# The scan's second round moved into the first group's end, and split products issued pass by pass

## The chip, the cores and the metric

The kernel runs on one core of a Trainium2 chip. The metric is device time in microseconds (us) of one execution. Before the change the median of 3 runs is 2160.34 us (2158.78 to 2164.11).

## The reference

One decoder layer runs over 2064 prompt positions (16 meta tokens and 2048 prompt tokens) and 8 short sequences of 8 tokens, model width 1024. All is float32. Cut to what matters:

```python
xn = rmsnorm(h, norm_gain);  proj = xn @ w_in          # u_s, z_s, u_p, z_p and two gates
dt = exp(log_dt);  abar = exp(dt * a)                   # 64 groups of 16 channels, 64 complex states each
s[t] = abar * s[t-1] + bbar @ u_s[t]                    # the linear scan over time (S5)
y_s = gelu(real(c @ s) + d * u_s);  y_s = y_s * sigmoid(y_s @ w_glu + b_glu)
y_p = ((window means of u_p) - u_p) @ pool_mix * pool_scale
merged = g_s * ((y_s * silu(z_s)) @ w_branch_ssm) + g_p * ((y_p * silu(z_p)) @ w_branch_pool)
out = rmsnorm(h + merged @ w_out)                       # and the final states of the scan
```

## The kernel before, in words

**Tiling.** Features lie on the 128 partitions, tokens along the free axis. The 2128 tokens are cut into four token groups g0 to g3 (`GROUPS`) of 544, 536, 536 and 512 columns; g0 drops its 16 meta tokens after the pooling inputs, so most of its products have 528 columns. In g0, g1 and g2 a product is too wide for one PSUM bank, so it has two token halves (`nh` = 2, 272, 268 or 264 columns); g3 has one of 512.

**Split products.** Each operand is kept as a high part and a low part in fp32r (`wh`, `wl` for weights, `ah`, `al` for activations). A product is three passes, high by high (L126), high weights by low activations (L127), low weights by high activations (L128), all added in the same PSUM tile `acc` (3 buffers). `mm3` issues the three for one half. `proj` goes over 8 blocks of 128 input features and calls `mm3` for each half: 48 matmuls for a group with two halves.

**Units.** The work is a written list of 339 units, most of them one `proj` with one block of 128x1024 weights. Around each unit the main loop converts the weights two units ahead (POOL writes `wh` at L103, DVE writes `wl` at L202), loads three units further, and issues the unit's *post* (the evacuation of `acc`) one unit later. Each engine runs its instructions in the order in which the loop issues them.

**Stages of a token group.** Pooling inputs and their gates (`up`, `zp`, `mix`), the pooling branch with its gate (`brp`, `gate`), the gate of the scan's branch (`zs`), `glu`, the scan's branch (`gate`, `brs`), and `out`. The scan's inputs (`us`) of all groups come early: g1 and g0 at the start, g2 and g3 in the middle of g0's work.

**The scan.** 64 channel groups are handled as 32 pairs, in two rounds: round 0 has the columns of g0 and g1 (135 steps of 8 tokens), round 1 those of g2 and g3 (123 steps and 8 sample sequences). A round is 37 *ticks*; in one tick six consecutive pairs are each moved on by one step. EARLY of a tick sits a quarter of its share into the unit, LATE at its end. Of the pair's steps, PE has L508 (into PSUM tile `sx`) and L573, L574 (into `sy`), float32 matmuls; ACT L499 to L501, L515, L516, L518, L542, L543 and L578 (`sy` to `sY`, one buffer, from which a DMA writes `ys`); DVE L495, L524, L533, L536 (twice), L553, L554; POOL L486, L489, L528, L563 to L566. `sx` and `sy` exist once each, so the next pair's matmul waits until the last one is evacuated.

**Where ticks go.** `spread` shares a round's 37 ticks out over a range of units, with weight `low` for units in the set `busy` and 1 elsewhere. Round 0 has one or two ticks in most units from g0's `brp` on (34 units). Round 1 starts in the first `gate` behind g0's `zs` and ends in g2's `brp`; the pooling units of g1 and g2 have weight `BB` = 0, and of the 12 + 20 + 5 ticks in g0, g1 and g2 a unit has at most one.

**Memory.** `to_ssm` opens the SBUF pool `sw` and the PSUM pool `ps` for the scan and keeps them to the end. `final_states` writes the final states out.

Of the kernel before, what the change touches and what calls it, by code (L numbers as in the profile page):

```python
# [15 lines left out]
PSUM = bass.MemoryType.PSUM  # L16
# [4 lines left out]
P = 128  # L21
# [36 lines left out]
XN = 5.5, 0.25  # L58
NPART = 2
LAST = 14  # L60
BA, BB = 0.25, 0.0
RAW = 3

BESIDE = [0] * 3 + [2] * 2 + [0] * 4 + [3] * 3 + [2] * 27
# [24 lines left out]
def hybrid_step(ctx, tc, a):  # L89
# [30 lines left out]
        flush()  # L120
        lows.append((l, x, h))

    def mm3(out, w, x, first, last):

        (wh, wl), (xh, xl) = w, x
        PE.matmul(out, wh, xh, start=first, stop=False)  # L126
        PE.matmul(out, wh, xl, start=False, stop=False)  # L127
        PE.matmul(out, wl, xh, start=False, stop=last)  # L128

    def rsqrt_mean(out, ss, r, q):  # L130

# [323 lines left out]
    sw = {}  # L455
# [148 lines left out]
    def between(part):  # L604

        while mid and mid[0][0] <= part:
            _, f, args = mid.pop(0)
            f(*args)


    class Group:
# [42 lines left out]
        def proj(self, w, xh, xl, halves=None, meta=False):  # L654


            ps = self.acc()
            n, km = (self.N, 0) if meta else (self.ND, self.km)
            if halves:
                n = self.HD  # L660
            strided = km and xh[0].shape[1] == self.C
            tn = T // self.nh
            nk = len(xh)
            for k in range(nk):
                between(k / nk)
                for h in halves or range(self.nh):
                    out = ps[:, h, :n]
                    if strided:
                        out = out.rearrange("p (t k) -> p t k", t=tn)
                        x = [v[k].rearrange("p (t k) -> p t k", t=T)[:, h * tn:(h + 1) * tn, km:]  # L670
                             for v in (xh, xl)]
                    else:
                        x = [v[k][:, h * n:(h + 1) * n] for v in (xh, xl)]
                    mm3(out, [x[:, k * P:(k + 1) * P] for x in w], x, k == 0, k == nk - 1)
            return ps

        def slot(self, pool, k, x, eng):
# [180 lines left out]
        def mix(self, wi, w):  # L858
            f0 = 2 * wi
            xh, xl = zip(self.pl.pop(f0), self.pl.pop(f0 + 1))  # L860
            pss = []
            for j in range(2):
                wj = []
                for x in w:
                    wj.append([x[:, k * 256 + j * P:k * 256 + (j + 1) * P] for k in range(2)])
                ps = self.acc()
                for k in range(2):
                    for h in range(self.nh):
                        c = slice(h * self.ND, (h + 1) * self.ND)
                        mm3(ps[:, h, :self.ND], (wj[0][k], wj[1][k]), (xh[k][:, c], xl[k][:, c]),  # L870
                            k == 0, k == 1)
                pss.append(ps)

            def post():
                for j in range(2):
                    fb = f0 + j
                    s = self.sz[fb]
                    V.scalar_tensor_tensor(self.v3(s), self.pv(pss[j]), psc16[:, fb:fb + 1], self.v3(s),  # L878
                                           ALU.mult, ALU.mult)
                for fb in (f0, f0 + 1):  # L880
                    self.yh[fb], self.yl[fb] = self.slot(self.sb, fb, self.sz.pop(fb), "a")
            return post
# [160 lines left out]
    def at(i, f, *args):  # L1043
        events.setdefault(max(i, 0), []).append((f, args))
# [29 lines left out]
    def u_pgate(g):  # L1074
        for f in range(NB):
            i = add("w", W_BRP + f, g.brp, f)
            if f + 3 < NB:
                add("w", W_GP + f + 3, g.gate, f + 3, 1)
        return i
# [72 lines left out]
    def spread(r, lo, hi, busy, low):  # L1152

        share = [low if i in busy else 1.0 for i in range(lo, hi)]
        total, done, n = sum(share), 0.0, 0
        for i, w in zip(range(lo, hi), share):
            done += w
            while n < NTICK and (n + 0.5) * total < done * NTICK:
                ticks.setdefault(i, []).append((r, n))
                n += 1  # L1160
# [22 lines left out]
    def to_ssm():  # L1183
        while beside():
            pass
        sw["g"] = ctx.enter_context(tc.tile_pool(name="gp", bufs=1))
        sw["p"] = ctx.enter_context(tc.tile_pool(name="sw", bufs=1))
        ps = ctx.enter_context(tc.tile_pool(name="ps", bufs=1, space=PSUM))
        for n in ("sx", "sy"):
            sw[n] = ps.tile([P, 2, 160], F32, name=n)  # L1190
        sw["xs"] = sw["p"].tile([P, GRP, NS], F32, name="xs")

    g0, g1, g2, g3 = grp
    for f in range(NB):
# [20 lines left out]
    i = len(units)  # L1215
# [5 lines left out]
    i = len(units)  # L1221
# [11 lines left out]
    for f in range(NB):  # L1233
# [7 lines left out]
        at(j, g0.y_split, f)  # L1241
        at(j + (f > 4), g0.y_gate, f)
    u_rest(g0, g1, 2)
    for g, nxt in ((g1, g2), (g2, g3), (g3, None)):
        n = len(units)
        u_pool(g)
        busy |= set(range(n, len(units)))
        hi = u_pgate(g)
        if g is g2:
            spread(rounds[1], i + 2, hi, busy, BB)  # L1250
        u_zs(g, range(NB), True)
        u_rest(g, nxt, 0)
    at(hi, final_states)


    V.memset(onesm, 1.0)
# [151 lines left out]
```

## Time and profile before

| | |
|---|---|
| median of 3 runs | 2160.34 us |
| the profiled execution | 2158.2 us, of which 2156.4 us is the span of its instructions |
| mean granted TensorE clock | 0.990 |
| HBM read, written | 242.32 MB, 40.62 MB |

The span is the time from the first to the last instruction of the profiled execution; busy time of an engine is counted within it. PE is TensorE's matmuls, PEld its weight loads, which overlap with matmuls, DVE VectorE, ACT ScalarE, POOL GpSimd, SP the queue that issues DMAs. A stretch is named by its start and end in us from the span's start. The units can be found in the trace by counting matmuls; they give these stretches:

| stretch, us | units | ticks |
|---|---|---|
| 290 to 577.5 | 34: g0's `brp` and `gate`, `zs` 0 to 4, `us` of g2 and g3 | 37 of round 0 |
| 577.5 to 805 | 35: the rest of g0 | 12 of round 1 |
| 805 to 930 | 23: g1's pooling inputs | none |
| 930 to 1286.5 | 53: the rest of g1 | 20 of round 1 |
| 1412.7 to 1482 | 11: g2's `brp` and `gate` | 5 of round 1 |
| 1482 to the end | 122: the rest of g2, and g3 | none |

### The profile page before, as it was taken

The page shows a single profiled execution, that of the slowest core. Times are in us where ns is not written, and L with a number is a line of the kernel's source. Part 1 is how long each engine was busy: PE and PEld are TensorE (multiplying, and loading weights), DVE is VectorE, ACT ScalarE, POOL GpSimd, SP SyncE. Part 2 cuts the span into 40 slices and gives each one's busy share as a digit, 9 for nine tenths or more (in the row PEclk, how much of TensorE's full clock was granted, in tenths as well). Part 3 has the DMA queues.
Part 4 walks back from the last instruction along what each step waited for, and adds up shares of the span by engine and source line. Part 5 has one row for each costly group of instructions (what it writes and reads, how often), then busy time and mean ns, then how long its engine had stood idle before and what let it go on. Part 6 is the DMA issues. An engine that isn't in the chain of part 4 may idle for free.

```text
span 2156.4 us, 37693 instructions
## 1 busy us (share of the span) xinstructions
PE 2084.8 (97%) x14968; PEld 1970.0 (91%) x14968; DVE 1395.2 (65%) x1916; ACT 686.5 (32%) x1243; POOL 931.2 (43%) x1054
## 2 busy tenths in 40 slices
PE   7999999889899999999999999999999999999998
PEld 7988899888799999999899999999999987888887
DVE  7889968978656686644856676634643767456444
ACT  3213357645444332144544332121210221112101
POOL 3387747655444452234644452233421333144222
PEclk9999999999999999999999999999999999999999
DMA  6646557586933543245444543234333433343233
GB/s 200 145 116 165 164 170 206 143 198 156 186 122 124 159 137 127 81 121 142 124 124 138 162 134 125 89 119 115 100 103 108 141 128 119 101 133 117 91 98 105
DMA packets 261279, 287.77 MB, mean 133 GB/s; under 512 B 106096, under 2 KB 203760, under 8 KB 261104
## 3 DMA queue, kind: packets, MB, share of 16 engines
q1 hardware_dynamic: 261104, 285.37, 45.8%
q8 instruction: 118, 1.93, 0.4%
q14 instruction: 57, 0.47, 0.1%
HBM read 242.32 MB, written 40.62 MB: 131 GB/s over the span
## 4 chain that ended last, share of the span: by engine, by line
PE 69%; DVE 7%; DMA 5%; ACT 3%; issue 2%; POOL 1%; SPq 0%; DVEq 0%; ACTq 0%; POOLq 0%
PE acc L126 22%; PE acc L128 22%; PE acc L127 22%; DMA ys<-sY 3%; DVE wl L202 1%; DVE sX L533 1%; DVE sph L554 1%; DVE sX L536 1%; PE sy L574 1%; PE sx L508 1%; DVE al L114 1%; PE sy L573 1%; DMA mat_d<-mp 1%; DVE sph L495 0%; ACT sXw L543 0%
## 5 line engine op out<-in xcount | busy, mean ns | idle before, releaser
L126 PE MATMUL acc<-ah,wh 128*128 128x268 f32 (+4 forms) x4504 | 1370.9, 304 | 8.9 <-ACT ah L698 6.6
L128 PE MATMUL acc<-ah,wl 128*128 128x268 f32 (+4 forms) x4504 | 1360.5, 302 | 4.8 <-DVE wl L202 4.8
L127 PE MATMUL acc<-al,wh 128*128 128x268 f32 (+4 forms) x4504 | 1359.0, 302 | 0.0
L126 PEld LDWEIGHTS acc<-ah,wh 128*128 128x128 f32 x4504 | 853.2, 189 | 43.2 <-issue 7.7
L128 PEld LDWEIGHTS acc<-ah,wl 128*128 128x128 f32 x4504 | 850.5, 189 | 33.1 <-DVE wl L202 5.9
L127 PEld LDWEIGHTS acc<-al,wh 128*128 128x128 f32 x4504 | 852.4, 189 | 27.5 <-issue 0.2
L103 POOL TENSOR_SCALAR wh<-raw 128x1024 fp32r<-128x1024 f32 (+1 forms) x336 | 395.9, 1178 | 964.2 <-PE acc L127 834.7
L202 DVE TENSOR_TENSOR wl<-raw,wh 128x1024 fp32r<-128x1024 f32 (+1 forms) x336 | 427.2, 1272 | 147.2 <-POOL wh L103 146.7
L890 ACT ACTIVATE sg<-acc,hb 128x536 f32<-128x536 f32 (+2 forms) x64 | 44.9, 702 | 404.0 <-PE acc L128 403.9
L524 DVE TENSOR_TENSOR sX<-sx,scc 128x270 f32<-128x270 f32 (+1 forms) x64 | 27.2, 424 | 106.5 <-ACT xs L518 66.3
L114 DVE TENSOR_TENSOR al<-H,ah 128x536 fp32r<-128x536 f32 (+3 forms) x96 | 88.4, 954 | 7.6 <-POOL ah L103 5.2
L946 DVE SCALAR_TENSOR_TENSOR H<-po,H 128x536 f32<-128x536 f32 (+2 forms) x32 | 25.4, 795 | 101.9 <-ACT po L944 101.9
L846 ACT ACTIVATE H<-acc 128x536 f32<-128x536 f32 (+2 forms) x64 | 39.0, 610 | 139.5 <-PE acc L128 139.1
L105 ACT ACTIVATE ah<-H 128x536 fp32r<-128x536 f32 (+3 forms) x80 | 50.7, 646 | 96.1 <-DVE H L878 77.4
L847 DVE SCALAR_TENSOR_TENSOR H<-H,acc 128x536 f32<-128x536 f32 (+2 forms) x64 | 44.8, 700 | 47.0 <-ACT H L846 46.5
L813 DVE TENSOR_TENSOR w<-E 128x483 f32<-128x483 f32 (+2 forms) x32 | 22.0, 687 | 74.2 <-POOL E L800 65.1
L573 PE MATMUL sy<-su,smc 128*128 128x135 f32 (+1 forms) x256 | 52.4, 286 | 18.1 <-ACT sY L578 15.1
L957 DVE SCALAR_TENSOR_TENSOR sg<-sg,acc 128x536 f32<-128x536 f32 (+2 forms) x32 | 22.4, 702 | 69.4 <-PE acc L128 69.4
L536 DVE TENSOR_TENSOR_SCAN sX<-r,state,sX 128x135 f32<-128x135 f32 (+1 forms) x128 | 65.6, 554 | 2.3
L944 ACT ACTIVATE po<-acc,hb 128x536 f32<-128x536 f32 (+2 forms) x32 | 22.5, 704 | 134.5 <-PE acc L128 134.5
L899 DVE SCALAR_TENSOR_TENSOR G<-sg,acc 128x536 f32<-128x536 f32 (+2 forms) x32 | 22.4, 700 | 64.2 <-PE acc L128 64.2
L574 PE MATMUL sy<-sS,smc 128*128 128x135 f32 (+1 forms) x256 | 53.4, 291 | 10.8 <-POOL sS L565 10.8
(232 smaller groups left out, 2271.0 us busy)
## 6 DMA issues: line engine op xcount, KB each, us to landing
raw<-in_wb SPq DMA_DIRECT2D x318, 512.0 KB, 3.8
smc<-mat_d SPq DMA_DIRECT2D x64, 256.0 KB, 4.1
smb<-mat_d SPq DMA_DIRECT2D x64, 128.0 KB, 3.2
xr<-in_xb SPq DMA_DIRECT2D x21, 268.0 KB, 4.3
H<-in_xb SPq DMA_DIRECT2D x19, 268.0 KB, 4.4
su<-us SPq DMA_DIRECT2D x32, 135.0 KB, 4.2
ys<-sY SPq DMA_DIRECT2D x32, 135.0 KB, 4.6
us<-po SPq DMA_DIRECT2D x16, 268.0 KB, 6.7
```

The costliest lines, as they stand in the source:

```text
L103: G.tensor_scalar(out, in_, 1.0, 0.0, ALU.mult, ALU.add)
L105: A.activation(out, in_, AF.Copy)
L114: V.tensor_tensor(l, x, h.bitcast(F32), ALU.subtract)
L126: PE.matmul(out, wh, xh, start=first, stop=False)
L127: PE.matmul(out, wh, xl, start=False, stop=False)
L128: PE.matmul(out, wl, xh, start=False, stop=last)
L202: V.tensor_tensor(l[:, c], r[:, c], h[:, c].bitcast(F32), ALU.subtract)
L536: V.tensor_tensor_scan(x[:, j], r8[:, i].to_broadcast([P, g.kp]), x[:, j], state[:, i], ALU.mult, ALU.add)
L573: PE.matmul(d["py"][:, j], d["m"][:, j, :P], d["u"][:, j], start=True, stop=False)
L574: PE.matmul(d["py"][:, j], d["m"][:, j, P:], d["S"][:, j], start=False, stop=True)
L847: V.scalar_tensor_tensor(self.v3(out), self.v3(out), 1.0, self.pv(ps), ALU.add, ALU.mult)
L890: A.activation(self.v3(s), self.pv(ps), AF.Tanh, scale=0.5, bias=hb[:, b, fb:fb + 1])
```

## The change

There are two edits. First, `mm3` takes all halves of a product at once: the first pass runs over both halves, then the second over both, then the third. For g3, and for the last units of g3's `out`, which have one half each, the order stays.

Second, round 1's 37 ticks are spread over the units from g0's `zs` 7 to `out` 6, the first 8 of the range with weight `BB` = 0.5. The ticks in g1 and g2 are gone. `final_states` comes at g1's first unit instead of g3's last `brp`, and one unit later `end_ssm` closes the scan's PSUM and SBUF pools. No later code takes memory from what they held.

```diff
--- before.py
+++ after.py
@@ -58,7 +58,7 @@
 XN = 5.5, 0.25
 NPART = 2
 LAST = 14
-BA, BB = 0.25, 0.0
+BA, BB = 0.25, 0.5
 RAW = 3
 
 BESIDE = [0] * 3 + [2] * 2 + [0] * 4 + [3] * 3 + [2] * 27
@@ -120,12 +120,16 @@
         flush()
         lows.append((l, x, h))
 
-    def mm3(out, w, x, first, last):
-
-        (wh, wl), (xh, xl) = w, x
-        PE.matmul(out, wh, xh, start=first, stop=False)
-        PE.matmul(out, wh, xl, start=False, stop=False)
-        PE.matmul(out, wl, xh, start=False, stop=last)
+    def mm3(outs, w, xs, first, last):
+
+
+        wh, wl = w
+        for out, (xh, _) in zip(outs, xs):
+            PE.matmul(out, wh, xh, start=first, stop=False)
+        for out, (_, xl) in zip(outs, xs):
+            PE.matmul(out, wh, xl, start=False, stop=False)
+        for out, (xh, _) in zip(outs, xs):
+            PE.matmul(out, wl, xh, start=False, stop=last)
 
     def rsqrt_mean(out, ss, r, q):
 
@@ -663,6 +667,7 @@
             nk = len(xh)
             for k in range(nk):
                 between(k / nk)
+                outs, xs = [], []
                 for h in halves or range(self.nh):
                     out = ps[:, h, :n]
                     if strided:
@@ -671,7 +676,9 @@
                              for v in (xh, xl)]
                     else:
                         x = [v[k][:, h * n:(h + 1) * n] for v in (xh, xl)]
-                    mm3(out, [x[:, k * P:(k + 1) * P] for x in w], x, k == 0, k == nk - 1)
+                    outs.append(out)
+                    xs.append(x)
+                mm3(outs, [x[:, k * P:(k + 1) * P] for x in w], xs, k == 0, k == nk - 1)
             return ps
 
         def slot(self, pool, k, x, eng):
@@ -865,10 +872,9 @@
                     wj.append([x[:, k * 256 + j * P:k * 256 + (j + 1) * P] for k in range(2)])
                 ps = self.acc()
                 for k in range(2):
-                    for h in range(self.nh):
-                        c = slice(h * self.ND, (h + 1) * self.ND)
-                        mm3(ps[:, h, :self.ND], (wj[0][k], wj[1][k]), (xh[k][:, c], xl[k][:, c]),
-                            k == 0, k == 1)
+                    cs = [slice(h * self.ND, (h + 1) * self.ND) for h in range(self.nh)]
+                    mm3([ps[:, h, :self.ND] for h in range(self.nh)], (wj[0][k], wj[1][k]),
+                        [(xh[k][:, c], xl[k][:, c]) for c in cs], k == 0, k == 1)
                 pss.append(ps)
 
             def post():
@@ -1184,11 +1190,15 @@
         while beside():
             pass
         sw["g"] = ctx.enter_context(tc.tile_pool(name="gp", bufs=1))
-        sw["p"] = ctx.enter_context(tc.tile_pool(name="sw", bufs=1))
-        ps = ctx.enter_context(tc.tile_pool(name="ps", bufs=1, space=PSUM))
+        sw["p"], sw["end"] = pool("sw")
+        ps, sw["endps"] = pool("ps", space=PSUM)
         for n in ("sx", "sy"):
             sw[n] = ps.tile([P, 2, 160], F32, name=n)
         sw["xs"] = sw["p"].tile([P, GRP, NS], F32, name="xs")
+
+    def end_ssm():
+        sw["endps"].close()
+        sw["end"].close()
 
     g0, g1, g2, g3 = grp
     for f in range(NB):
@@ -1241,16 +1251,17 @@
         at(j, g0.y_split, f)
         at(j + (f > 4), g0.y_gate, f)
     u_rest(g0, g1, 2)
+
+
+    n = len(units)
+    spread(rounds[1], i + 2, n - 1, set(range(i + 2, i + 10)), BB)
+    at(n, final_states)
+    at(n + 1, end_ssm)
     for g, nxt in ((g1, g2), (g2, g3), (g3, None)):
-        n = len(units)
         u_pool(g)
-        busy |= set(range(n, len(units)))
-        hi = u_pgate(g)
-        if g is g2:
-            spread(rounds[1], i + 2, hi, busy, BB)
+        u_pgate(g)
         u_zs(g, range(NB), True)
         u_rest(g, nxt, 0)
-    at(hi, final_states)
 
 
     V.memset(onesm, 1.0)
```

On PE, at the end of g0 (`brs` and `out`), in the order before: the three passes of one half stand together, and a tick's scan matmuls (L573, L574, L508) stand between two units.

```order
L127 MATMUL acc<-al,wh 128x264
L128 MATMUL acc<-ah,wl 128x264
L573 MATMUL sy<-su,smc 128x131
L574 MATMUL sy<-sS,smc 128x131
L573 MATMUL sy<-su,smc 128x131
L574 MATMUL sy<-sS,smc 128x131
L508 MATMUL sx<-su,smb 128x131 x2
L126 MATMUL acc<-ah,wh 128x264
```

The same part now, in the middle of a unit with two ticks (L128, L130 and L132 are the three passes, L577, L578 and L512 the scan):

```order
L130 MATMUL acc<-al,wh 128x264 x2
L132 MATMUL acc<-ah,wl 128x264 x2
L577 MATMUL sy<-su,smc 128x131
L578 MATMUL sy<-sS,smc 128x131
L577 MATMUL sy<-su,smc 128x131
L578 MATMUL sy<-sS,smc 128x131
L512 MATMUL sx<-su,smb 128x131 x2
L128 MATMUL acc<-ah,wh 128x264 x2
```

Each pass now has two matmuls in a row with the same weights (x2), and a unit can have a tick's six scan matmuls both in its middle and at its end.

On DVE, one unit of g0's `out` before: the evacuation (L973), normalised inputs of g1 and their low parts (L752, L114), and the low weights for a later unit (L202).

```order
L973 SCALAR_TENSOR_TENSOR G_4104<-acc,xr 128x528
L752 SCALAR_TENSOR_TENSOR H_8378<-H_8378,sm,rs 128x536
L752 SCALAR_TENSOR_TENSOR H_8494<-H_8494,sm,rs 128x536
L114 TENSOR_TENSOR al<-H_8378,ah 128x536
L114 TENSOR_TENSOR al<-H_8494,ah 128x536
L202 TENSOR_TENSOR wl<-raw,wh 128x1024
```

The same unit now:

```order
L979 SCALAR_TENSOR_TENSOR G_4104<-acc,xr 128x528
L759 SCALAR_TENSOR_TENSOR H_8950<-H_8950,sm,rs 128x536
L759 SCALAR_TENSOR_TENSOR H_9198<-H_9198,sm,rs 128x536
L114 TENSOR_TENSOR al<-H_8950,ah 128x536
L114 TENSOR_TENSOR al<-H_9198,ah 128x536
L528 TENSOR_TENSOR sX<-sx,scc 128x246
L557 TENSOR_TENSOR scc<-scc,sX 128x2x123
L558 TENSOR_TENSOR sph<-sph,sXw 128x2x123
L537 TENSOR_TENSOR sX<-sX,sXw 128x246
L540 SCALAR_TENSOR_TENSOR sX<-r_69,state,sX 128x123 x2
L206 TENSOR_TENSOR wl<-raw,wh 128x1024
```

A tick's scan instructions (L528 to L540, the scans are the row with x2) now stand between the unit's evacuation and its low weights.

On ACT, in g0's `out`, before: evacuations and high parts, and one tick among them.

```order
L983 ACTIVATE po<-G_3715 128x528
L105 ACTIVATE ah<-H_7782 128x536
L105 ACTIVATE ah<-H_7898 128x536
L578 ACTIVATE sY<-sy 128x262
L542 ACTIVATE sXw<-sX 64x246
L543 ACTIVATE sXw<-sX 64x246
L515 ACTIVATE sXw<-sx 64x246
L516 ACTIVATE sXw<-sx 64x246
L518 ACTIVATE xs<-sx 128x16
L499 ACTIVATE scc<-sph 128x272
L500 ACTIVATE scc<-scc,halfpi 128x272
L501 ACTIVATE sph<-sph,sscale 128x272
```

The same place now:

```order
L582 ACTIVATE sY<-sy 128x262
L546 ACTIVATE sXw<-sX 64x246
L547 ACTIVATE sXw<-sX 64x246
L519 ACTIVATE sXw<-sx 64x246
L520 ACTIVATE sXw<-sx 64x246
L522 ACTIVATE xs<-sx 128x16
L503 ACTIVATE scc<-sph 128x272
L504 ACTIVATE scc<-scc,halfpi 128x272
L505 ACTIVATE sph<-sph,sscale 128x272
L582 ACTIVATE sY<-sy 128x262
L546 ACTIVATE sXw<-sX 64x246
L547 ACTIVATE sXw<-sX 64x246
```

Two ticks follow each other here, and the second one's evacuation into `sY` (L582) comes nine instructions after the first.

## Rows read from the trace of the kernel before

**Rows 1.** Page, part 1: busy time, share of span, instructions.
```profile
PE 2084.8 (97%) x14968; PEld 1970.0 (91%) x14968; DVE 1395.2 (65%) x1916; ACT 686.5 (32%) x1243; POOL 931.2 (43%) x1054
```

**Rows 2.** Stretches: each engine’s busy us (instructions), clock, DMA share, GB/s.
```profile
core 0: us, PE busy (x) PEld busy (x) DVE busy (x) ACT busy (x) POOL busy (x), PEclk, DMA share, GB/s
290.00:577.50 287.50, 258.02 (x1830) 242.66 (x1831) 229.23 (x331) 168.53 (x334) 167.26 (x236) 0.98 0.70 174
577.50:805.00 227.50, 221.47 (x1789) 220.51 (x1788) 152.53 (x188) 87.49 (x160) 114.25 (x127) 0.99 0.48 140
805.00:930.00 125.00, 125.00 (x1014) 124.87 (x1013) 78.16 (x131) 24.83 (x46) 32.10 (x40) 1.00 0.31 103
930.00:1286.50 356.50, 348.24 (x2788) 346.84 (x2787) 228.19 (x300) 160.18 (x293) 172.95 (x223) 0.99 0.47 137
1412.70:1482.00 69.30, 69.30 (x566) 69.30 (x565) 24.23 (x34) 14.91 (x30) 21.83 (x29) 1.00 0.39 118
1541.60:1588.90 47.30, 47.30 (x387) 47.30 (x386) 15.47 (x16) 5.59 (x8) 10.62 (x9) 1.00 0.31 101
1683.90:1731.70 47.80, 47.80 (x387) 47.80 (x386) 32.18 (x35) 10.31 (x16) 19.72 (x14) 1.00 0.46 144
1967.00:2011.10 44.10, 44.10 (x192) 35.85 (x191) 14.62 (x16) 5.41 (x8) 10.47 (x9) 1.00 0.32 107
930.15:937.38 7.23, 7.23 (x62) 7.23 (x61) 5.76 (x10) 5.86 (x12) 6.02 (x9) 1.00 0.46 130
```

**Rows 3.** Waits of PE, 290 to 577.5: us in total, times, longest.
```profile
PE sx L508 <- DVE sX L524: 9.0, 9, 2.2
PE sy L573 <- ACT sY L578: 8.7, 4, 3.8
PE sy L574 <- POOL sS L565: 4.7, 6, 1.6
PE acc L739 <- DVE rs L716: 2.9, 2, 2.2
```

**Rows 4.** Waits of ACT, same stretch.
```profile
ACT sY L578 <- DMA ys<-sY: 38.7, 14, 6.3
```

**Rows 5.** Groups by line, DVE, same stretch: busy us, mean ns, idle before.
```profile
L202 DVE TENSOR_TENSOR wl<-raw,wh 128x1024 fp32r<-128x1024 f32 x34 | 46.2, 1359 | 1.8 <-POOL wh L103 1.8
L536 DVE TENSOR_TENSOR_SCAN sX<-r,state,sX 128x135 f32<-128x135 f32 x64 | 37.2, 622 | 1.1
L554 DVE TENSOR_TENSOR sph<-sph,sXw 128x270 f32<-128x270 f32 x32 | 27.5, 859 | 1.6 <-ACT sXw L543 1.6
L533 DVE TENSOR_TENSOR sX<-sX,sXw 128x270 f32<-128x270 f32 x32 | 26.6, 832 | 0.0
L553 DVE TENSOR_TENSOR scc<-scc,sX 128x270 f32<-128x270 f32 x32 | 20.2, 630 | 0.0
L495 DVE SCALAR_TENSOR_TENSOR sph<-scc,sph 128x272 f32<-128x272 f32 x32 | 19.4, 605 | 9.0 <-POOL scc L489 9.0
L524 DVE TENSOR_TENSOR sX<-sx,scc 128x270 f32<-128x270 f32 x32 | 14.0, 437 | 40.2 <-ACT sXw L516 40.1
```

**Rows 6.** Groups by line, DVE, 1493.8 to 1731.7.
```profile
L202 DVE TENSOR_TENSOR wl<-raw,wh 128x1024 fp32r<-128x1024 f32 x40 | 48.6, 1215 | 23.5 <-POOL wh L103 23.5
```

**Rows 7.** Groups by shape, PEld, whole span.
```profile
L126 PEld LDWEIGHTS acc<-ah,wh 128*128 128x128 f32 x4504 | 853.2, 189 | 43.2 <-issue 7.7 <-POOL wh L103 6.5 <-POOL craw L378 1.8
L127 PEld LDWEIGHTS acc<-al,wh 128*128 128x128 f32 x4504 | 852.4, 189 | 27.5 <-issue 0.2 <-DVE al L699 0.2
```

**Rows 8.** Timeline, PE, 1553.0 to 1553.4: start, us, engine, instruction.
```profile
1553.07 0.28 PE L126 MATMUL acc<-ah,wh 128*128 128x268 f32 x1
1553.19 0.28 PE L127 MATMUL acc<-al,wh 128*128 128x268 f32 x1
1553.31 0.28 PE L128 MATMUL acc<-ah,wl 128*128 128x268 f32 x1
```

**Rows 9.** Groups by line, POOL, 1915 to 1960.
```profile
L599 POOL TENSOR_TENSOR xs<-xs,s 128x512 f32<-128x512 f32 x2 | 2.9, 1454 | 0.2
```

## The prediction

> **What bounds the kernel now.** I read the page's busy times first. PE is busy for 2084.8 of 2156.4 us [rows 1], so the reader should look for the few places where it is not. The table of stretches shows them [rows 2]: in the two that hold most ticks PE's busy time falls short of the stretch, by 29.5 us from 290 to 577.5 (287.50 against 258.02) and by 8.3 us from 930 to 1286.5, while stretches without ticks are full to the last tenth. So the kernel is bound by PE, and what PE loses it loses to the scan. The waits of PE say how: matmuls into `sx` wait for DVE to evacuate it (9.0 us), matmuls into `sy` for ACT (8.7) and for POOL's states (4.7) [rows 3]. Each is the end of a chain over four engines, and PE stands in the middle of a unit when it waits. Behind ACT stands a DMA: `sY` has one buffer, and ACT waited 38.7 us for the store of the last pair to land [rows 4].
>
> **Prices.** Eight `glu` units without a tick take 47.30 us and eight `out` units 47.80 [rows 2], so a unit of two halves is 5.91 to 5.98, and I use 5.94. A unit of g3 is 44.10 / 8 = 5.51. A unit with one tick that waits for nothing took 7.23 [rows 2] against 5.97 (47.80 / 8), so a tick costs PE 1.26 us even when all is ready.
>
> **The ticks taken away.** From 930 to 1286.5 there are 53 units and 20 ticks. Without ticks they need 53 x 5.94 = 314.8 us, so 356.5 - 314.8 = 41.7 us come back. From 1412.7 to 1482 there are 11 units with the last 5 ticks: 69.3 - 65.3 = 4.0 us. Together 45.7 us, of which 25 x 1.26 = 31.5 are plain work that only moves; 14.2 are stalls and lost clock.
>
> **The ticks added.** The rest of g0 is 35 units, 35 x 5.94 = 207.9 us without ticks; it takes 227.5 now with 12 ticks. With all 37 and no stall it would take 207.9 + 37 x 1.26 = 254.5 us. How much stall comes on top is not shown for this stretch, but the nearest row is round 0, which has the same 37 ticks in 34 units. Its 26 units of two halves and 8 of one need 26 x 5.94 + 8 x 5.51 = 198.5 us, with the ticks 245.1, and it took 287.5 [rows 2]. That is 42.4 us of stalls, of which 2.9 belong to a row norm that the rest of g0 hasn't [rows 3]; 39.5 us remain, and clock lost after pauses (granted 0.98 there) is in them.
>
> Will the new stretch stall as much? The load on DVE says at least that. In round 0 a pair cost DVE 37.2 + 27.5 + 26.6 + 20.2 + 19.4 + 14.0 = 144.9 us over 32 pairs, 4.53 each [rows 5]; a pair of round 1 has 123 steps for 135, so about 4.1. The rest of g0 has DVE busy for 152.5 us with 12 ticks [rows 2]; 25 more make 152.5 + 103 = 255.5, against 254.5 us that PE needs without a stall. In round 0 it was 229.2 against 245.1. The spacing of ticks is alike too: round 0 has seven units with two ticks, the rest of g0 gets eight, and two ticks in one unit lie (5.94 + 2 x 1.26) / 2 = 4.2 us apart on PE in both. ACT and POOL, at 168.5 and 167.3 us in round 0, come second on each count. On the other side, round 0 shares its stretch with the input norms of g2 and g3, which the rest of g0 hasn't. I take round 0's 39.5 us as they are: 207.9 + 46.6 + 39.5 = 294.0 us, 66.5 more than now.
>
> The ends: no stall at all gives 254.5 us, +27.0. If DVE is the limit and is busy for the share that round 0 had, 229.2 / 287.5 = 0.797, the stretch takes 255.5 / 0.797 = 320.5 us, +93.0.
>
> **The order of the passes.** It removes no instruction. In the trace each matmul has its own weight load, also L127, which follows L126 with the same `wh`: 4504 loads each of 189 ns [rows 7]. Matmuls start 0.12 us apart whether the weights are new (L127 to L128) or repeated (L126 to L127), and whether the PSUM half changes or not [rows 8]. So I cost it at 0. The nearest rows for an error in that are the 5.91 and 5.98 us that equal units take with operands in different places; 246 units of two halves times 0.03 us is 8 us either way, and both ends stay in the range. `wl` is wanted two matmuls later, 0.25 us, which matters only where PE waits for it.
>
> The Trainium skill, "TensorE: Matmul & The Clock Gate", Back-to-back issue gap, says that in a stream of weight loads and matmuls the spacing is set by both. By its figure for a matmul alone, N / 2.4 + 2.5 ns, 268 columns would take an estimated 114 ns where the row has 123 (47.30 us / 384), so if repeated weights cost no load, some 5,900 matmuls would save an estimated 53 us. No run here shows a load that was dropped.
>
> **The rest.** `final_states` is two additions of 1.45 us on POOL [rows 9] and as many products, under 6 us, and its two loads; at its new place POOL is busy for 32.1 of 125 us and weights are two units ahead, so 0. If that cover were gone, PE would wait those 6 us. The freed memory is taken by nothing: 0.
>
> **The sum.** -45.7 + 66.5 + 0 = +20.8 us. The profiled execution took 2158.2 (span 2156.4 and 1.8 around it), so 2179.0; the median of the runs is 2.1 above that execution: 2181 us. Below, 2.1 is added in the same way.
>
> **The rivals.**
>
> *No stall.* The ticks find everything ready as most of the sparse ones do now, and the stretch takes 254.5 us: 2158.2 + 27.0 - 45.7 + 2.1 = 2142 us, faster. For it: of the 45.7 us that 25 sparse ticks take now, 31.5 are plain work; DVE has a whole stretch to average over, and `busy` thins the ticks where `glu` needs its low parts. Against it: round 0. It decides as long as DVE reaches each evacuation of `sx` before PE does.
>
> *DVE is the limit.* 320.5 us for the stretch: 2208 us, slower still. For it: 255.5 us of DVE work in a stretch that PE could do in 254.5. Against it: some of round 0's idle time on DVE was its input norms. It is low weights, low parts of `brs` and `out` and the scan that queue behind each other on DVE. `wl` took 1359 ns in round 0 and 1215 in a stretch without ticks [rows 5, 6], so DVE's work also grows when the scan is beside it. The Trainium skill, "SBUF — State Buffer", Who interferes with whom, has a reason: a VectorE instruction with two SBUF inputs and a GpSimd instruction that reads SBUF lock each other out. By that rule, with which these rows agree, more POOL work in the stretch would push it towards this rival.
>
> *The repeated weights are cheaper.* From 512 and 268 columns (44.10 us / 192 = 229.7 ns and 123.2 ns) the part of a matmul that doesn't grow with columns is 123.2 - 268 x 106.5 / 244 = 6.2 ns. If the second matmul of each pass (5,904 of them) lost all of it, 37 us would go: 2144 us with my other terms. Against it: [rows 7, 8].
>
> *Half hidden.* Stalls of about 20 us instead of 39.5 leave 2161 us, no change.
>
> **How the numbers follow.** My forecast 0.50 (its own range 2167 to 2200), DVE as the limit 0.12, no stall 0.25, half hidden 0.09, cheap repeats 0.04. A measurement here tells 0.3%, 6.5 us, from no change. Faster is no stall and cheap repeats, less what falls inside the bound: 0.28. Slower is the forecast and the DVE limit, less the forecast's low edge: 0.60. The same: 0.12. The range reaches from the no-stall case with 8 us for the passes and a little more, 2132, to just above the DVE limit, 2212.
>
> **What would show it.** Right: from about 577 us a stretch of some 290 us up to g0's end, with PE waiting for `sx` and `sy` as in round 0, ACT waiting for the store of `ys`, half-clock pieces, and DVE busy for some 80 to 90% of it; then g1 and g2 at 5.91 to 5.98 us a unit throughout. Step by step: a g1 from 930 on that is not 40 us shorter breaks the first term; a rest of g0 under 265 us breaks the second; units without ticks off 5.91 to 5.98 us by more than 0.05 break the zero for the passes. The forecast is wrong if PE passes the ticks of a two-tick unit without waiting.

## The result, and the profile after

The changed kernel takes 2185.31 us (median of 4 runs, 2181.64 to 2188.89) against 2160.32 (2158.78 to 2164.11). The ratio is 1.0113, 95% interval 1.0092 to 1.0134. The forecast was slower, 2181 us. The profiled execution has a span of 2183.3 us, 26.9 more than before.

The page's busy times answer to [rows 1]:

```profile
PE 2094.7 (96%) x14968; PEld 1975.9 (91%) x14968; DVE 1387.1 (64%) x1916; ACT 656.4 (30%) x1218; POOL 935.6 (43%) x1054
```

No matmul or load of weights was added or taken away. ACT has 25 instructions and 30 us less: its table loads fell from 82 to 57 at 1283 ns each.

The table of stretches answers to [rows 2], with the same columns. The first line is the whole rest of g0, then follow its unit 86, units 87 to 96 and units 97 to 107, g1 behind its pooling, eight `glu` and eight `out` units of g1:

```profile
576.80:879.80 303.00, 268.15 (x2065) 262.05 (x2064) 236.36 (x341) 176.74 (x371) 207.69 (x285) 0.95 0.55 154
664.20:681.50 17.30, 11.19 (x76) 10.58 (x74) 15.40 (x22) 12.27 (x26) 14.62 (x20) 0.80 0.43 116
681.50:767.00 85.50, 78.81 (x639) 77.28 (x638) 67.61 (x112) 59.30 (x132) 65.83 (x102) 1.00 0.64 181
767.00:879.80 112.80, 92.23 (x662) 89.07 (x662) 85.76 (x124) 49.22 (x115) 67.24 (x95) 0.89 0.54 150
1005.40:1319.40 314.00, 314.00 (x2547) 314.00 (x2546) 147.30 (x159) 50.24 (x78) 95.21 (x84) 1.00 0.35 113
1129.80:1177.20 47.40, 47.40 (x387) 47.40 (x386) 14.85 (x16) 5.58 (x8) 10.70 (x10) 1.00 0.30 101
1271.90:1319.40 47.50, 47.50 (x387) 47.50 (x386) 32.03 (x35) 10.46 (x16) 19.35 (x15) 1.00 0.43 141
```

g1 behind its pooling falls from 356.5 to 314.0 us and PE is busy in all of it; 11 units of g2 fall from 69.3 to 65.1. The rest of g0 grows from 227.5 to 303.0. Its 35 units and 37 ticks need 254.5 us without a stall, so 48.5 us are stall. Subtracting 5.94 us and 1.26 per tick from each unit puts 8.8 of them in unit 86 (two ticks), 9.1 in the two-tick units 89, 93 and 96, 22.4 in the two-tick units 99, 102 and 105, 1.1 in unit 83, the only two-tick unit in `glu`, and 10.1 in the single-tick units 97, 98, 100, 101, 103 and 104; the other units are 3 us under. PE is idle for 34.9 of the 303.0 us. The granted clock of 0.95 means some 30 us at the lower level, 1.2 GHz, in units 86, 99, 102 and 105, in and behind PE's pauses there; PE was busy for 23.6 us of that time, so matmuls at half speed are some 12 us of the stall.

The waits of PE in the rest of g0 answer to [rows 3], the waits of ACT to [rows 4] (us in total, times, longest):

```profile
PE sy L578 <- POOL sS L569: 11.6, 6, 3.8
PE sx L512 <- DVE sX L528: 11.5, 11, 3.5
PE sy L577 <- ACT sY L582: 7.4, 4, 3.5
PE sy L577 <- DMA smc<-mat_d: 3.2, 3, 1.6
```

```profile
ACT po L989 <- DVE G L979: 28.0, 6, 5.8
ACT sY L582 <- DMA ys<-sY: 23.5, 10, 4.8
ACT sXw L546 <- DVE sX L540: 17.0, 13, 4.8
```

In the rest of g0 PE waits for the same three engines as in round 0. New is the first line of ACT: the Square of a finished row block of `out` waits for DVE's sum. ACT's part of unit 102 shows what that does (start, us, engine, instruction, idle before it and its releaser):

```profile
822.07 0.64 ACT L989 ACTIVATE po<-G 128x528 f32<-128x528 f32 x1 [3.97 <-DVE G L979]
822.76 1.34 ACT L105 ACTIVATE ah<-H 128x536 fp32r<-128x536 f32 x2
824.00 0.37 ACT L582 ACTIVATE sY<-sy 128x262 f32<-128x262 f32 x1
```

The evacuation of `sy` stands behind the Square, and PE waited 3.49 us for it. DVE in the same place:

```profile
820.22 1.20 DVE L206 TENSOR_TENSOR wl<-raw,wh 128x1024 fp32r<-128x1024 f32 x1
821.34 0.70 DVE L979 SCALAR_TENSOR_TENSOR G<-acc,xr 128x528 f32<-128x528 f32 x1
821.96 1.46 DVE L759 SCALAR_TENSOR_TENSOR H<-H,sm,rs 128x536 f32<-128x536 f32 x2
823.44 2.33 DVE L114 TENSOR_TENSOR al<-H,ah 128x536 fp32r<-128x536 f32 x2
826.23 0.41 DVE L528 TENSOR_TENSOR sX<-sx,scc 128x246 f32<-128x246 f32 x1 [0.46 <-ACT xs L522]
```

DVE works without a pause through `wl`, the sum, g1's row norm and its low parts before it reaches the next evacuation of `sx`.

DVE's groups in the rest of g0 answer to [rows 5]; `wl` takes longer than in any stretch shown before:

```profile
L206 DVE TENSOR_TENSOR wl<-raw,wh 128x1024 fp32r<-128x1024 f32 x35 | 49.7, 1421 | 1.9 <-POOL wh L103 1.9
L540 DVE TENSOR_TENSOR_SCAN sX<-r,state,sX 128x123 f32<-128x123 f32 x64 | 39.8, 662 | 1.1
L528 DVE TENSOR_TENSOR sX<-sx,scc 128x246 f32<-128x246 f32 x32 | 13.2, 413 | 35.3 <-ACT xs L522 35.2
```

The new order of the passes, which answers to [rows 8], and the loads in the eight `glu` units, which answer to [rows 7] (each of the three passes has one load for each matmul, 187 to 188 ns):

```profile
1130.05 0.40 PE L130 MATMUL acc<-al,wh 128*128 128x268 f32 x2
1130.29 0.41 PE L132 MATMUL acc<-ah,wl 128*128 128x268 f32 x2
1130.54 0.41 PE L128 MATMUL acc<-ah,wh 128*128 128x268 f32 x2
```

```profile
L128 PEld LDWEIGHTS acc<-ah,wh 128*128 128x128 f32 x130 | 20.3, 187 | 0.0
L130 PEld LDWEIGHTS acc<-al,wh 128*128 128x128 f32 x128 | 19.9, 188 | 0.0
```

Pairs start 0.245 us apart, 0.1225 a matmul. Taken singly over the eight units, a matmul with repeated weights starts 123.4 ns behind the one ahead of it and one with new weights 123.3 ns. The two additions of `final_states`, for [rows 9], take 1.3 us each at their new place, and nothing waits there.

### The profile page after: what moved, and what is told of

Same layout as the page of the kernel before. It is cut to its first block, busy times and chain, and to the rows that moved or that the text cites. A ratio compares the mean times of both kernels' runs of the same rounds, so it can differ in the third digit from the quotient of the medians.

```text
span 2183.3 us, 37850 instructions
## 1 busy us (share of the span) xinstructions
PE 2094.7 (96%) x14968; PEld 1975.9 (91%) x14968; DVE 1387.1 (64%) x1916; ACT 656.4 (30%) x1218; POOL 935.6 (43%) x1054
## 4 chain that ended last, share of the span: by engine, by line
PE 67%; DVE 7%; DMA 4%; issue 3%; ACT 3%; POOL 3%; SPq 1%; DVEq 0%; POOLq 0%; ACTq 0%
PE acc L128 22%; PE acc L130 22%; PE acc L132 22%; DMA ys<-sY 2%; DVE wl L206 1%; DVE sph L558 1%; DVE sX L540 1%; DVE sX L537 1%; DMA xr<-in_xb 1%; DMA H<-in_xb 1%; DVE sph L499 1%; PE sy L578 1%; DVE al L114 1%; DVE sX L528 0%; ACT sXw L547 0%
## 5 line engine op out<-in xcount | busy, mean ns | idle before, releaser
L128 PE MATMUL acc<-ah,wh 128*128 128x268 f32 (+4 forms) x4504 | 1059.7, 305 | 8.9 <-ACT ah L705 6.5
L132 PE MATMUL acc<-ah,wl 128*128 128x268 f32 (+4 forms) x4504 | 1049.7, 303 | 3.7 <-DVE wl L206 3.7
L130 PE MATMUL acc<-al,wh 128*128 128x268 f32 (+4 forms) x4504 | 1049.0, 302 | 0.5 <-DVE al L114 0.5
L103 POOL TENSOR_SCALAR wh<-raw 128x1024 fp32r<-128x1024 f32 (+1 forms) x336 | 382.1, 1137 | 968.6 <-PE acc L130 857.8
L128 PEld LDWEIGHTS acc<-ah,wh 128*128 128x128 f32 x4504 | 730.3, 190 | 44.7 <-issue 7.2
L132 PEld LDWEIGHTS acc<-ah,wl 128*128 128x128 f32 x4504 | 729.1, 190 | 32.1 <-DVE wl L206 4.8
L130 PEld LDWEIGHTS acc<-al,wh 128*128 128x128 f32 x4504 | 729.2, 190 | 27.9 <-DVE al L114 0.9
L114 DVE TENSOR_TENSOR al<-H,ah 128x536 fp32r<-128x536 f32 (+3 forms) x96 | 84.5, 914 | 8.6 <-POOL ah L103 6.2
L540 DVE TENSOR_TENSOR_SCAN sX<-r,state,sX 128x135 f32<-128x135 f32 (+1 forms) x128 | 77.2, 644 | 2.3
L528 DVE TENSOR_TENSOR sX<-sx,scc 128x270 f32<-128x270 f32 (+1 forms) x64 | 27.2, 425 | 73.1 <-ACT sXw L520 37.6
L577 PE MATMUL sy<-su,smc 128*128 128x135 f32 (+1 forms) x256 | 53.6, 291 | 19.4 <-ACT sY L582 12.5
L532 POOL TENSOR_TENSOR sXw<-sXw,sph 128x270 f32<-128x270 f32 (+1 forms) x64 | 43.9, 685 | 66.0 <-ACT sXw L520 51.1
L578 PE MATMUL sy<-sS,smc 128*128 128x135 f32 (+1 forms) x256 | 54.5, 296 | 15.6 <-POOL sS L569 15.5
L963 DVE SCALAR_TENSOR_TENSOR sg<-sg,acc 128x536 f32<-128x536 f32 (+2 forms) x32 | 22.4, 701 | 68.9 <-PE acc L132 68.9
```

What stands on the lines that cost most here:

```text
L103: G.tensor_scalar(out, in_, 1.0, 0.0, ALU.mult, ALU.add)
L114: V.tensor_tensor(l, x, h.bitcast(F32), ALU.subtract)
L540: V.tensor_tensor_scan(x[:, j], r8[:, i].to_broadcast([P, g.kp]), x[:, j], state[:, i], ALU.mult, ALU.add)
L577: PE.matmul(d["py"][:, j], d["m"][:, j, :P], d["u"][:, j], start=True, stop=False)
L578: PE.matmul(d["py"][:, j], d["m"][:, j, P:], d["S"][:, j], start=False, stop=True)
```

## The experiments

All times are medians; the kernel before ran beside each and had 2159.7 to 2160.3. The diffs are cut to the lines that carry the change. The kernels with their own places for ticks also have `final_states` and `end_ssm` behind the last tick. Unit times are read from each run's trace by counting matmuls.

**passes_only**: the kernel before with the new `mm3` and its two callers, and nothing else of the diff.

```diff
+        for out, (xh, _) in zip(outs, xs):
+            PE.matmul(out, wh, xh, start=first, stop=False)
+        for out, (_, xl) in zip(outs, xs):
+            PE.matmul(out, wh, xl, start=False, stop=False)
```

> The kernel before with only the new order of the passes; the scan's second round stays sparse. If the passes are free, the time is that of before within 8 us: units of two halves at 5.92 us each as in the changed kernel, against 5.91 and 5.98, so some 2 us less, 2158. If repeated weights were cheaper, 37 us or more would go (2123 or less). If the passes carry part of the slowdown, the time would lie well above 2167.

Measured 2157.32, ratio 0.9983 (0.9975 to 0.9991). The new order of the passes saves some 2.7 us by itself.

**move_only**: the changed kernel with the old order inside `mm3`.

```diff
-        for out, (xh, _) in zip(outs, xs):
+        for out, (xh, xl) in zip(outs, xs):
             PE.matmul(out, wh, xh, start=first, stop=False)
-        for out, (_, xl) in zip(outs, xs):
             PE.matmul(out, wh, xl, start=False, stop=False)
-        for out, (xh, _) in zip(outs, xs):
             PE.matmul(out, wl, xh, start=False, stop=last)
```

> The changed kernel with the old order of the passes (each half's three matmuls together) and the moved second round. Theory: the whole slowdown is the move, 2185 to 2189 us, with the rest of g0 at about 303 us and g1 without stalls. Rival: if the slowdown needs both edits, this kernel lies near 2160.

Measured 2187.71, ratio 1.0122 (1.0108 to 1.0137). The whole slowdown comes with the second edit, the move of the ticks.

**no_store**: round 1's `ys` isn't stored.

```diff
-        SY.dma_start(chans(g, ys_d, q), y)
+        if not g.last:
+            SY.dma_start(chans(g, ys_d, q), y)
```

> The changed kernel without the store of round 1's scan outputs: g2 and g3 read round 0's outputs in their place, in the same number and size of loads. ACT's evacuation into the single buffer sY then never waits for a store to land. Theory of the store (the 23.5 us that ACT waits there set the pace of the units with two ticks): the rest of g0 falls from 303 to some 275 us, 2155 to 2165 in all. Theory of the chain (two ticks in one unit leave PE, ACT, DVE and POOL too little time for the way from sx through the scan to sy, and each engine's queue stands in that way): at most the 7.4 us that PE waits for ACT's evacuation and the 1.7 us per half-clock piece go, 2170 to 2180.

Measured 2177.76, ratio 1.0078 (1.0062 to 1.0094): 7.5 us less than the changed kernel. Units 89, 93 and 96 fell from 11.1 to 11.9 us to 8.6, 8.6 and 9.6; units 86, 99, 102 and 105 kept 14.2 to 18.0. So the store is one cause, in the two-tick units of `brs` and `gate`, and not the main one: the 23.5 us that ACT waited for it are gone, but ACT's waits for DVE's scan (`sXw` from `sX`) rose from 17.0 to 25.0.

**one_per_unit**: round 1's ticks one in each of units 75 to 111.

```diff
-    spread(rounds[1], i + 2, n - 1, set(range(i + 2, i + 10)), BB)
+    for k in range(NTICK):
+        ticks.setdefault(i + 2 + k, []).append((rounds[1], k))
```

> The changed kernel with round 1's ticks laid one in each unit from g0's zs 7 on, 37 units in a row, so that no unit has two; the last 5 fall into g1's pooling inputs. The ticks per us are nearly as many as in the changed kernel. Theory of the chain or of the store (the stalls come from two ticks in one unit): nearly all stalls go, a tick costs 1.26 us, and the time is 2140 to 2150, faster than before. Theory of DVE as the limit (too much work per us, however it is spaced): DVE works some 235 us within these units, and at the share it reached (0.78) that needs about 300 us; the time stays at 2175 to 2185.

Measured 2173.93, ratio 1.0059 (1.0045 to 1.0073), 11.4 us less. In units 79 to 85 and 88 to 98 each tick cost about 1.26 us and nothing more; units 77, 78, 86, 87 and 99 to 109 stalled. The time lies just under the range of DVE as the limit and well above that of the chain: no unit has two ticks here, so most `glu` and `brs` units do as the theory of the chain says, but the `out` units stall all the same.

**pairs**: one_per_unit with 16 ticks put two by two, in 80, 82, 84, 88, 90, 92, 94 and 96.

```diff
+    where = [75, 76, 77, 78, 79, 80, 80, 82, 82, 84, 84, 86, 87,
+             88, 88, 90, 90, 92, 92, 94, 94, 96, 96, *range(98, 112)]
```

> The kernel one_per_unit (round 1's ticks one per unit in units 75 to 111, 2173.9 us) with 16 of its ticks put two by two: units 80, 82, 84, 88, 90, 92, 94 and 96 hold two ticks and the unit behind each holds none. In these units single ticks cost 7.2 to 7.35 us without a stall, and DVE, ACT and POOL get the same work over the stretch. Theory A (two ticks in one unit lie too near for the chain over four engines): each two-tick unit takes 11 to 12 us, as units 89, 93 and 96 of the changed kernel, where a unit with two ticks and no stall would take 8.5; 8 x 2.6 to 3.5 us, so 2195 to 2202 us. Theory B (the load of an engine decides, and it is the same): 8.5 us for each two-tick unit and 2170 to 2178 us in all.

Measured 2185.39, ratio 1.0114 (1.0097 to 1.0130): 11.5 us more, between the two. Most two-tick units took 9.5 us where 8.5 were due, not 11 to 12. The stretch table shows it, units 88 to 98 of one_per_unit ahead and 88 to 97 of pairs behind:

```profile
689.50:769.50 80.00, 80.00 (x664) 80.00 (x662) 59.43 (x103) 54.83 (x117) 55.96 (x91) 1.00 0.67 194
```

```profile
699.50:777.70 78.20, 74.38 (x602) 73.24 (x602) 56.84 (x94) 49.59 (x106) 47.06 (x81) 1.00 0.60 172
```

The second line has ten ticks in ten units, the first eleven in eleven. DVE has 5.7 us of work a unit for 5.4, ACT 5.0 for 5.0 and POOL 4.7 for 5.1, yet PE, idle nowhere before, is now idle for 3.8 us. In those units PE waits 2.7 us for DVE's evacuation of `sx` (5 times), and ahead of that evacuation DVE waits 11.2 us for ACT's `xs` (6 times). ACT in unit 94 of pairs says why:

```profile
752.54 0.39 ACT L582 ACTIVATE sY<-sy 128x262 f32<-128x262 f32 x1 [4.60 <-DMA ys<-sY]
753.61 0.41 ACT L546 ACTIVATE sXw<-sX 64x246 f32<-64x246 f32 x1 [0.67 <-DVE sX L540]
```

The second tick's `sY` waits for the store of the first, and ACT's other steps of that tick, `xs` among them, wait behind it.

**late_square**: one_per_unit with ACT's Square of g0's `out` issued late in the next unit, behind its tick.

```diff
+                if self.gi > 0:
+                    square()
+            if g.gi == 0:
+                at_part(i + 1, 0.8, lambda: g0.square())
```

> one_per_unit (2173.9 us) with one change in g0's out units: ACT's Square of the finished row block is issued at the end of the next unit's tick instead of ahead of it. In one_per_unit ACT waited 30.2 us at this Square for DVE's sum, with the tick's evacuations queued behind it. Theory A (a waiting instruction at the head of ACT's queue holds the tick's steps up): of the some 21 us that units 99 to 108 take beyond 5.94 + 1.26 each, 12 or more go, so 2153 to 2162 us. Theory B (DVE has too much work in out, 81 per cent busy there): no change, 2170 to 2178 us.

Measured 2164.90, ratio 1.0023 (1.0013 to 1.0032): 9.0 us less, short of the 12 that were expected. Units 101, 102 and 107 fell to 7.2 to 7.4 us; 103 to 105, which hold g1's row norm, stayed at 10.1 to 10.9.

**late_both**: late_square with that row norm behind the tick too.

```diff
-                    at(i, nxt.x_norm, 2 * f - 4)
-                    at(i, nxt.x_norm, 2 * f - 3)
+                    for k in (2 * f - 4, 2 * f - 3):
+                        if g.gi == 0:
+                            at_part(i, 0.85, nxt.x_norm, k)
```

> late_square (2164.9 us) with one more change: in g0's out units the row norm of g1's rows (x_norm, a product on DVE and a rounding on ACT) is issued behind the unit's tick instead of ahead of it. In late_square units 103 to 105 still take 10.1 to 10.9 us; in the trace ACT waits there 5.2 us for this product on DVE, with the tick's evacuations of sY and sX behind it in its queue. Theory A (an instruction of other work that waits at the head of ACT's queue): units 103 to 105 fall to 7.2 to 8.5 us, 2154 to 2158 us in all. Theory B (DVE's total work in out): it is the same, so 2162 to 2167 us.

Measured 2166.10, ratio 1.0024 (1.0013 to 1.0035): no change. Unit 103 fell to 8.1, unit 106 rose to 10.2. Its stretch of units 99 to 107 with a little on either side:

```profile
768.00:856.00 88.00, 75.29 (x600) 73.71 (x599) 79.06 (x113) 45.24 (x113) 57.68 (x82) 0.98 0.59 166
```

With the Square and the row norm behind ACT's steps of the tick, DVE is busy for 90% of the stretch. In units 99 to 107 alone (771.0 to 851.1) DVE's work is 72.9 us, where PE needs 9 x (5.94 + 1.26) = 64.8. So a tick in every one of these units is more than DVE can do in PE's time.

**after_late**: the changed kernel with both moves of late_both.

```diff
+            if g.gi == 0:
+                at_part(i + 1, 0.8, lambda: g0.square())
+                        if g.gi == 0:
+                            at_part(i, 0.85, nxt.x_norm, k)
```

> The changed kernel (2185.3 us) with its own order of ticks, two in units 99, 102 and 105 among them, and with both moves of late_both: in g0's out units ACT's Square and g1's row norm are issued behind the tick. Units 97 to 105 hold 32.7 of the 48.5 us by which the rest of g0 exceeds 254.5 us without a stall. Theory A (head of ACT's queue): half of that or more goes, 2157 to 2169 us. Theory C (two ticks in one unit are too near whatever stands around them): it stays in units 99, 102 and 105, 2177 to 2186 us.

Measured 2184.57, ratio 1.0112 (1.0097 to 1.0128): no change, as theory C had it and against theory A. Unit 102 fell from 16.8 to 11.6 us, but 105 kept 15.5, 99 14.2, and 86 17.9.

**no_low**: the changed kernel without the subtraction that makes `wl` in units 76 to 107.

```diff
+        if same:
+            splits[key] = (h, h)
+            return
```

> The changed kernel (2185.3 us) without the low part of the weights of units 76 to 107: DVE's subtraction that makes wl (some 1.25 us each, 32 of them) is left out, and the third pass of these units multiplies by wh again, so PE, ACT, POOL and the ticks do the same work in the same order and the output leaves the low part out. In the changed kernel the rest of g0 has 48.5 us of stall: 31.1 in units 97 to 107 (DVE busy 85.8 us there, PE's own need 81.7), 9.7 in 87 to 96 (DVE 67.6, PE 75.8), 8.8 in unit 86. Theory B (DVE's load): with 14 us of DVE's work gone from units 97 to 107 (72 against 81.7) their stall falls by 15 us or more, and the time to 2150 to 2168 us. Theory C (two ticks in one unit are too near for the chain of steps over four engines, whatever the load): units 86, 99, 102 and 105 stay at 14 to 17 us, 2176 to 2186 us.

Measured 2167.73, ratio 1.0035 (1.0025 to 1.0045): 17.6 us less, at the upper end of what the load theory gave. Unit 86, units 87 to 96 and units 97 to 107 in the table:

```profile
664.50:680.60 16.10, 10.87 (x74) 10.23 (x73) 12.96 (x20) 11.55 (x26) 13.42 (x20) 0.79 0.44 116
680.60:760.90 80.30, 78.01 (x638) 77.11 (x637) 50.21 (x102) 59.48 (x132) 53.03 (x102) 1.00 0.67 191
760.90:862.00 101.10, 87.62 (x664) 85.41 (x663) 73.67 (x114) 49.19 (x115) 64.52 (x95) 0.93 0.62 168
```

Units 97 to 107 fell by 11.7 us, less than the 15 that were expected of them, and 87 to 96 by 5.2. Some 29 us of the 48.5 stay, and 28 of them in the two-tick units: 86 at 16.1 us, 99 at 13.1, 102 at 15.2, 105 at 13.9, 89, 93 and 96 at 9.3 to 10.1. In units 97 to 107 DVE now has 73.7 us of work, less than the 81.7 that PE needs, and 19.4 us of stall stay. So less load eases the stall and does not cure two ticks in one unit. The subtraction also stood in DVE's queue ahead of evacuations; this run takes away its time and its place at once, and can't tell the two apart.

**clean_units**: the changed kernel with round 1 one tick per unit, only where a single tick had cost 1.26 us: 19 ticks in the rest of g0 and 18 in g1.

```diff
+    where = [*range(79, 86), *range(87, 99), *range(131, 143), *range(152, 158)]
+    for k, u in enumerate(where):
+        ticks.setdefault(u, []).append((rounds[1], k))
```

> The changed kernel (2185.3 us) with round 1's 37 ticks one per unit in units where a single tick cost 1.26 us in some run: 79 to 85 and 87 to 98 (rest of g0), 131 to 142 and 152 to 157 (brp, gate and glu of g1). Theory A (the place decides): all 37 cost 1.26 us, the 99 units of the three stretches take 588.1 + 46.6 = 634.7 us where before took 653.2, and with 2.7 us from the passes the time is about 2139 us (2134 to 2146). Theory B (a tick in every unit in a row overloads an engine): stalls as in one_per_unit, 2160 to 2175 us.

Measured 2135.17, ratio 0.9883 (0.9868 to 0.9898), as the theory of the place had it. Units 88 to 98, then 131 to 142, with a tick in every unit:

```profile
675.20:755.20 80.00, 80.00 (x663) 80.00 (x662) 63.40 (x105) 54.89 (x117) 57.47 (x92) 1.00 0.69 196
933.60:1020.80 87.20, 87.20 (x721) 87.20 (x720) 56.61 (x107) 61.44 (x128) 52.34 (x98) 1.00 0.61 169
```

**both_spaced**: clean_units with round 0 one tick per unit as well, from 39 to 74 (two in 39).

```diff
-    spread(rounds[0], lo, i, busy, BA)
+    for k in range(NTICK):
+        ticks.setdefault(lo + max(k - 1, 0), []).append((rounds[0], k))
```

> clean_units with round 0's ticks too one per unit: two in unit 39, one each in 40 to 74, instead of seven units with two and six with none in 39 to 74. Theory A (two ticks in a unit are what stalls): the seven two-tick units of round 0 took some 33 us beyond their plain units, 24 of it stall; most of that goes, so 2112 to 2128 us. Theory B (round 0 stalls from the load on DVE, which stays): within 5 us of clean_units.

Measured 2122.64, ratio 0.9825 (0.9811 to 0.9840), within the range of theory A and the fastest of all.

**both_early**: both_spaced with seven two-tick units instead, and no tick in 53, 54, 64 and behind 71.

```diff
+    early = [u for u in range(39, 72) if u not in (53, 54, 64)] + [42, 44, 46, 48, 50, 57, 67]
+    for k, u in enumerate(sorted(early)):
+        ticks.setdefault(u, []).append((rounds[0], k))
```

> both_spaced (2122.6 us) with round 0's ticks placed otherwise: none in units 53, 54 and 64 (row norms of g2 and g3) and none after 71, where single ticks took 8.9 to 10.3 us; seven units of g0's brp and gate and of us hold two instead (42, 44, 46, 48, 50, 57, 67). If the place decides, the six units that lose a tick give back some 14 us of stall and the two-tick units cost 1 to 2 us each: 2108 to 2120 us. If two ticks in a unit cost what they cost in round 0 before, 3 to 4 us of stall each: 2120 to 2135 us.

Measured 2132.86, ratio 0.9871 (0.9856 to 0.9886): 10.2 us more than both_spaced. Units 44, 46, 48, 50, 57 and 67 took 11.7 to 15.1 us, a stall of 3 to 7 where 3 to 4 were expected at worst. Unit 42 took 8.2 us, without a stall; it holds the round's first ticks, in which fewer than six pairs move.

## Why the prediction was right

*The ticks taken away*, 45.7 us: measured 42.5 in g1 and 4.2 in g2, 46.7 together. Right; the passes are little of it, since in passes_only g1 fell by 0.6 us.

*The ticks added*, 66.5 us: measured 75.5. The plain part, 46.6, stands: where a tick waited for nothing it cost about 1.26 us in every kernel. The term that was mis-sized is the stall, 48.5 for the 39.5 taken over from round 0. The rest of g0 hasn't the input norms of g2 and g3, and it did not stall less for that; its `out` units have the Square, the sum and g1's row norm in the same queues, and round 0 has no `out` units. Moving the Square gave 9.0 us with single ticks (late_square) and nothing clear in the changed kernel (after_late), so this is a likely reason, not a shown one. The two terms together miss by 8 us and the time by only 4: the other units came out 1.9 us shorter, and the 2.1 us that I added for the median were 0.2. That 39.5 us, measured among other work, came within a fifth of 48.5 is in part luck.

*The mechanism.* I took the stalls over from round 0, where PE waits at the end of a chain over four engines with the store of `sY` behind it, and counted two-tick units as what makes the stretches alike. That two ticks lie too near for this chain is part of it. Leaving round 1's store out took 7.5 us away, and pairs and both_early show two-tick units stalling where single ticks at nearly the same average load don't. The other part is the load on DVE, which I priced as a rival of its own: taking `wl` out gave 17.6 us. These two effects lie over one another, so they can't be added, and no_low leaves open whether DVE's time or its queue counts. How the stall of units 86, 99, 102 and 105 divides among the store, the queue of ACT and DVE stays open; removing any one of them left each of the four at 11.6 to 18 us.

*DVE is the limit*, 2208 us: as a rule over the whole stretch it was wrong (DVE busy for 236.4 of 303.0 us, 78%). Its 255.5 us of work were too many: I priced each of the 25 added ticks as one pair, 4.1 us, but 37 ticks move 32 pairs, and an added tick measured 3.4. In units 97 to 107 DVE has 85.8 us of work where PE needs 81.7, which my average over the stretch hid; by itself that accounts for 4.1 of the 31.1 us of stall there.

*No stall*, 2142 us: clean_units has no stall in round 1 with the same 37 ticks and the changed pools, at 2135.2, but with half of them in g1. So the places decide, and the rest of g0 has clean places for 19 at least. No run has all 37 there without a stall: one_per_unit and late_both, with 33 of them there one by one, still stall in `out`.

*The passes*, 0 with 8 us either way: 2.7 us gained. In passes_only 49 units that took 5.97 us take 5.92 on average and 47 that took 5.91 take 5.93; why is not shown. That a change of the PSUM half costs nothing either is not in the three lines of [rows 8], but it is so: in the eight `glu` units before, the step from L128 to L126, where the half changes, is 123 to 124 ns, and the other steps are 121 to 124. *Cheap repeats*, 2144 us, is out: each matmul still loads its weights, and a repeat starts as late as a new one (123.4 and 123.3 ns). The Trainium skill, "TensorE: Matmul & The Clock Gate", Back-to-back issue gap, has the spacing in a stream set by load and matmul both. The 0.1225 us here, the same for repeats, agree with that, and the 53 us estimated from its figure for a matmul alone were not to be had.

*Half hidden*, 2161 us: missed by 28 us of stall. `final_states` and the memory were 0 as costed. Of the signs that I named, PE's waits, ACT's wait for the store, the lower clock and the full g1 are there; the stretch is 303 us for some 290, and DVE is at 78%, just under the 80 to 90% I gave. The sign of being wrong came close in one unit: PE passed the two ticks of unit 83 with 1.1 us of stall.

## What to carry to other kernels

When a second stream of short dependent steps is threaded through a loop that PE bounds, price each place and not the stretch: look for the unit whose engines already hold a long run of in-order work (a norm, a set of low parts, a Square that waits for a sum) and put nothing there. One step per unit in quiet units cost only its own matmuls, in every kernel here; two in a unit mostly cost 1 to 10 us of stall, even at nearly the same average load (none in units 41 and 42, with the round's first ticks, and 0.1 us in units 89 and 93 once the store was left out). Before a move of work into a shorter stretch, compare the busiest other engine with PE's own need unit by unit, since an average of 78% hid a place where DVE's work was 105% of PE's need.

## What was not expected of the hardware

A pause costs more than itself. Unit 86 of the changed kernel was granted 0.80 and units 97 to 107 0.89; the rest of g0 as a whole has some 12 us of its 48.5 us of stall in matmuls at 1.2 GHz. In clean_units the stretches with round 1's ticks show 1.00.

DVE's subtraction for `wl` has the same shape everywhere and took 1215 ns without ticks beside it [rows 6], 1359 in round 0 [rows 5] and 1421 in the changed stretch. It does not follow the number of ticks: in units 88 to 98 of clean_units, with a tick in each, it took 1234 ns. The traces show what it follows. Of the 35 in the changed stretch, 15 began while POOL was idle and took 1193 to 1226 ns; 20 began while a POOL instruction ran, 15 of them took 1575 to 2344 ns, and the other 5 began with 132 ns or less of a POOL instruction left and took 1193 to 1212. An example:

```profile
697.84 1.61 DVE L206 TENSOR_TENSOR wl<-raw,wh 128x1024 fp32r<-128x1024 f32 x1
697.62 0.75 POOL L490 TENSOR_TENSOR sph<-pA,pB 128x272 f32<-128x272 f32 x1
698.46 1.27 POOL L493 TENSOR_SCALAR scc<-sph 128x272 f32<-128x272 f32 x1
```

`wl` began 0.22 us behind L490 and took 0.4 us more than without it. L493, which began while `wl` ran, took 1.27 us, where it took 0.42 to 0.46 in unit 102 with no `wl` beside it. Here each instruction that began while the other engine's was running is the longer for it.
